# Attention pieces and the projections beside them, issued by a list in the kernel; step projection joined to the values

## The chip, the cores and the metric

The kernel runs on one core of a Trainium2 chip. A core has a matrix engine (TensorE, "PE" in the profile, with its weight loads as "PEld"), VectorE ("DVE"), ScalarE ("ACT"), GpSimd ("POOL") and SyncE ("SP", which here issues nearly all DMAs). Each engine takes its own queue of instructions in the order in which the program was built and stops at an instruction whose semaphores are not there yet. The metric is the device time of one execution in microseconds.

## The reference

One layer of a hybrid diffusion backbone on 512 latent tokens of width 1024, with 256 context tokens. What matters here:

```python
p_lat = h_lat @ w_in                  # columns: z 2048 | xBC 3072 | dt 64 | q 1024 | k 256 | v 256 | gates 2048
p_ctx = h_ctx @ w_in
dt = softplus(dt_raw + dt_bias)       # 2 directions x 32 heads: the "steps" of the state-space scan
q_l, k_l = axial_rope(q), axial_rope(k)
# per block of 128 queries, per KV head (4 query heads each):
logits = concat([q k_win / 8 (+-128 tokens), q k_ctx / 8, sink])
o = softmax(logits) @ [v_win, v_ctx]  # 16 heads of 64, 4 KV heads
out = (sig(g_ssd) * (ssd @ w_o_ssd) + sig(g_att) * (att @ w_o_att)) @ w_out
# then gated residual, ConvFFN, gated residual, final RMSNorm
```

## The kernel before

All large products are made in split precision. A weight piece (128 x 1024, float32, tile `wraw`) is loaded on SP's queue, cast by ACT to `whi` (L149) and its residual made by DVE as `wlo` (L150). `gemm` then issues three matmuls for each of eight slices of the inner dimension: `whi` by the high part, `whi` by the low part, `wlo` by the high part (L192, L193, L195), for 512 latent or 256 context columns. `load` has two buffers each of `whi` and `wlo` and three of `wraw`; `run` goes through a list of steps and loads one piece ahead.

The kernel goes through stages: modulation and norm; keys, queries and values; attention with the z projections beside it; the gates of z, the attention output product (`oa_step`) and the tables of the steps; the state-space scan; the merge; the FFN. The change lies between the values and the attention output product.

Keys and queries. `k_step` and `q_step` make 128 output rows, `rope` rotates them (four quarter copies on ACT, three operations on DVE). `split_k` and `q_split` split the result into high and low halves of a 128-partition tile, by half-tile copies on ACT (L590, L613) and half-tile subtractions on DVE (L591, L614), so that one matmul over 128 partitions multiplies both halves of a query (64 rows high, 64 rows low) by keys doubled on both halves.

Values. `v_step` makes values in token order for six tiles of 128 tokens: 6 tiles x 8 slices x 3 matmuls of 256 columns (L627 to L629), then ACT copies the high part (L634) and DVE makes the residual (L635) in `vst`.

Attention. `block(j, b)` handles KV head j and query block b, 16 in all. For each of four heads: the scores (L669: keys high, keys low, for window and context; into one buffer `score` of two PSUM banks), a masked minimum on DVE (L676, which frees the score buffer), the exponential with its sum on ACT (L680). Then the sums and reciprocals for four heads (L683 to L686), scaling in place on ACT (L689) and DVE (L691). Then for each of 4 or 5 key tiles: four transposes (L698, tile `pt`), high part on ACT (L701), residual on DVE (L702), and two products with the values (L703, L704, tile `po`). At the end ACT copies half of `po` (L706) and DVE adds (L710).

Between blocks stand whole steps: one K step, six Q steps and z steps, given by a table:

```python
    with_ = {(0, 2): [k_step(1)]}
    for j in range(3):
        for b in range(2):
            with_[j, b] = [q_step(2 * j + 2 + b)]
```

A z step (`z_step`) is one product of 512 columns, a tanh on ACT (L520), a multiply on DVE (L522) and a store to DRAM. The framework's scheduler decides how the instructions of neighbouring steps are interleaved on each engine, from its own model of costs, and sets the semaphores.

Steps ("dt"). `dt_tables` first makes its own product with a weight piece of 64 output rows (`gemm(..., m=64)`, 48 matmuls), adds the bias, and computes tables in a long chain of operations on DVE and ACT. It stands behind `att_split` (the split of the attention result into `atth` and `attl`, L837 and L838), three z steps and the first output product; `dt_turn` uses the tables behind the last output product.

Of the kernel before, what the change touches and what calls it, by code (L numbers as in the profile page):

```python
# [44 lines left out]
def tile_hybrid_layer(  # L45
# [14 lines left out]
    wdt: bass.AP,  # L60
# [59 lines left out]
    src["dt", 0] = wdt, 512  # L120
    for i in range(2):
        src["k", i] = wk[i], 1024
        src["v", i] = wv[i], 1024
# [97 lines left out]
    cs_d = dpool.tile([64, L], F32, name="cs_d")  # L221
    tt_d = dpool.tile([64, 4], F32, name="tt_d")
# [351 lines left out]

    def rope(ps, scale):
        sw = tmp("ta")
        for d, s in ((0, 32), (32, 0), (64, 96), (96, 64)):
            S.activation(sw[d : d + 32, :], ps[s : s + 32, :], AF.Copy, scale=scale)
        r = tmp("tb")
        V.scalar_tensor_tensor(r, ps, scale, cosb, ALU.mult, ALU.mult)  # L580
        V.tensor_tensor(sw, sw, sinb, ALU.mult)
        V.tensor_tensor(r, r, sw, ALU.add)
        return r

    def split_k(r, t, lo, hi):
        n = hi - lo
        for u in range(2):
            a, j = 64 * u, 2 * t + u
            for b in (0, 64):
                S.copy(khi[b : b + 64, j, lo:hi], r[a : a + 64, :n])  # L590
                V.tensor_tensor(klo[b : b + 64, j, lo:hi], r[a : a + 64, :n], raw(khi[b : b + 64, j, lo:hi]), ALU.subtract)  # L591

    def k_step(t):
        def fn(w):
            pl, pc = accb(), accb()
            gemm([LAT(pl)], w)
            gemm([CTX(pc)], w)
            split_k(rope(pl, -0.125), t, 0, L)
            rc = tmp("tc")
            S.activation(rc[:, :LC], pc[:, :LC], AF.Copy, scale=-0.125)  # L600
            split_k(rc, t, L, 768)

        return [("k", t)], fn

    Q = {}

    def q_split(ps, t):
        r = rope(ps, 1.0)
        for u in range(2):

            a, b = 64 * u, 64 - 64 * u
            q = a2p.tile([P, L], F32R, tag="q", name="q", bufs=7)
            S.copy(q[a : a + 64, :], r[a : a + 64, :])  # L613
            V.tensor_tensor(q[b : b + 64, :], r[a : a + 64, :], raw(q[a : a + 64, :]), ALU.subtract)  # L614
            Q[2 * t + u] = q

    def v_step(*w):

        pos = [misb() for _ in range(3)]
        for k in range(KT):  # L620
            wh, wl = (z[:, (k % 4) * 256 : (k % 4 + 1) * 256] for z in w[k // 4])
            for p, po in enumerate(pos):
                hh, hl, c0 = (hlh, hll, 2 * p) if p < 2 else (hch, hcl, 0)
                for t in range(2):
                    c = slice((c0 + t) * P, (c0 + t + 1) * P)
                    o = po[:, t * 256 : (t + 1) * 256]
                    T.matmul(o, hh[:, k, c], wh, start=k == 0 and t == 0, stop=False, skip_group_check=True)  # L627
                    T.matmul(o, hh[:, k, c], wl, start=False, stop=False, skip_group_check=True)
                    T.matmul(o, hl[:, k, c], wh, start=False, stop=k == KT - 1, skip_group_check=True)  # L629
        for p, po in enumerate(pos):  # L630
            for t in range(2):
                o = po[:, t * 256 : (t + 1) * 256].rearrange("p (h d) -> p h d", h=4)
                v = vst[:, 2 * p + t, :, :]
                S.copy(v[:, :, 0:64], o)  # L634
                V.tensor_tensor(v[:, :, 64:128], o, raw(v[:, :, 0:64]), ALU.subtract)  # L635
# [11 lines left out]
    run([q_step(1), ([("v", 0), ("v", 1)], v_step)])  # L647
# [3 lines left out]
    def block(j, b, mid=None):  # L651
# [3 lines left out]
        order = con + lat if b == 3 else lat + con  # L655
        n = len(order) * P
        o0 = P if n == 640 else 0
        m = winm[:, 0:512] if b == 3 else winm[:, 896 - n :]
        mneg = a2p.tile([P, 4], F32, tag="mneg", name="mneg", bufs=2)
        den = a2p.tile([P, 4], F32, tag="den", name="den", bufs=2)  # L660
        pts = []
        for i in range(4):
            h = 4 * j + i
            ps = bank("score")
            o = o0
            for z in (con, lat) if b == 3 else (lat, con):
                w = len(z) * P
                for v, k in enumerate((khi, klo)):
                    T.matmul(  # L669
                        ps[:, o : o + w], Q[h][:, b * P : (b + 1) * P], k[:, j, z[0] * P : z[0] * P + w],  # L670
                        start=v == 0 and o % 512 in (0, P), stop=v == 1, skip_group_check=True,
                    )
                o += w
            p = a2p.tile([P, 640], F32, tag="p", name="p", bufs=7)
            mn = mneg[:, i : i + 1]
            V.tensor_tensor_reduce(  # L676
                p[:, :n], ps[:, o0 : o0 + n], m, op0=ALU.add, op1=ALU.min, scale=1.0, scalar=nsink[:, h : h + 1],
                accum_out=mn,
            )
            S.activation(p[:, :n], p[:, :n], AF.Exp, bias=mn, scale=-1.0, accum_out=den[:, i : i + 1])  # L680
            pts.append(p)
        es = a2p.tile([P, 4], F32, tag="es", name="es", bufs=2)
        V.tensor_tensor(es, bcs[:, 32 + 4 * j : 36 + 4 * j], mneg, ALU.add)  # L683
        S.activation(es, es, AF.Exp)
        V.tensor_tensor(es, es, den, ALU.add)
        V.reciprocal(es, es)  # L686
        for i in range(4):
            if i % 2:
                S.activation(pts[i][:, :n], pts[i][:, :n], AF.Copy, scale=es[:, i : i + 1])  # L689
            else:  # L690
                V.tensor_scalar(pts[i][:, :n], pts[i][:, :n], es[:, i : i + 1], None, ALU.mult)  # L691
        if mid:
            mid()
        po = bank("po")
        for c, t in enumerate(order):
            pt = bank("pt")
            for i in range(4):
                T.transpose(pt[:, i * P : (i + 1) * P], pts[i][:, c * P : (c + 1) * P], ident)  # L698
            pth = a2p.tile([P, L], F32R, tag="pth", name="pth", bufs=2)
            ptl = a2p.tile([P, L], F32R, tag="ptl", name="ptl", bufs=2)  # L700
            S.copy(pth, pt)  # L701
            V.tensor_tensor(ptl, pt, raw(pth), ALU.subtract)  # L702
            T.matmul(po, vst[:, t, j, :], pth, start=c == 0, stop=False)  # L703
            T.matmul(po, vst[:, t, j, :], ptl, start=False, stop=c == len(order) - 1)  # L704
        o2 = tmp("tc")
        S.copy(o2[0:64, :], po[64:128, :])  # L706
        po4 = po[0:64, :].rearrange("p (t u q) -> p u t q", t=2, u=2)
        o24 = o2[0:64, :].rearrange("p (t u q) -> p u t q", t=2, u=2)
        for u in range(2):
            V.tensor_tensor(att[64 * u : 64 * u + 64, 2 * j : 2 * j + 2, b * P : (b + 1) * P], po4[:, u], o24[:, u], ALU.add)  # L710
        if b == 3 and j == 0:
            dump("att", att[:, 0, :])

    F = {}
    fill = [z_step(i) for i in range(16)] + [g_step(i) for i in range(NG, 16)]
    n1, n2, n3 = 12, 15, 25

    with_ = {(0, 2): [k_step(1)]}
    for j in range(3):
        for b in range(2):  # L720
            with_[j, b] = [q_step(2 * j + 2 + b)]
# [799 lines left out]
```

## Time and profile before

| | us |
|---|---|
| median of 3 runs | 1292.05 (1290.18 to 1292.60) |
| profiled execution | 1290.21 |
| its span, first to last instruction | 1288.3 |
| PE busy in the span | 1255.9 (97%) |
| DVE busy | 904.5 (70%) |
| ACT busy | 664.7 (52%) |

The profiled execution is the one from which all rows come. Its time is 1.9 us more than its span; the median of the runs is 1.8 us more than its time. In a row of groups, the columns are line, engine, operation, output<-inputs, shape, count, then busy time in us, mean duration in ns, and the idle time of the engine just before, with what ended it. In a timeline row they are start, duration, engine, line, operation, names and count, with the idle time before it in brackets. Ends of matmuls are modelled, and starts are measured: two neighbours' starts tell the pace.

### The profile page before, as it was taken

How to read it: one execution, taken by the hardware profiler on the slowest of the kernel's cores; microseconds unless marked ns; L12 is line 12 of the kernel's file. 1: busy time of each engine (PE TensorE's matmuls, PEld its weight loads, DVE VectorE, ACT ScalarE, POOL GpSimd, SP SyncE). 2: the span in 40 equal slices, each digit the busy share in tenths (PEclk: the TensorE clock that was granted, in tenths of full speed). 3: DMA queues.
4: the chain of work that ended last, by engine and by line, in shares of the span. 5: the costliest groups of instructions: out<-in, count | busy, mean ns of one | idle time of the engine just before them, and what ended most of it. 6: DMA issues, size and time to landing. Idle time of an engine off the chain costs nothing.

```text
span 1288.3 us, 17234 instructions
## 1 busy us (share of the span) xinstructions
PE 1255.9 (97%) x6450; PEld 1022.2 (79%) x6450; DVE 904.5 (70%) x1439; ACT 664.7 (52%) x1230; POOL 132.9 (10%) x113
## 2 busy tenths in 40 slices
PE   7999999999999999999999999999999999999997
PEld 4698777887778878778687787888988888888886
DVE  3867888778495588887887767777677777773323
ACT  3568888767434456375564754223544444442221
POOL 0000000000000033432343430000200000000000
PEclk9999999999999999999999999999999999999999
DMA  8621112121335245444455558777133433333331
GB/s 335 244 92 50 41 58 66 66 74 66 99 127 184 82 107 147 139 119 133 142 131 188 155 168 291 242 244 237 46 113 115 132 114 114 104 109 102 91 102 66
DMA packets 86900, 168.66 MB, mean 131 GB/s; under 512 B 6753, under 2 KB 42081, under 8 KB 86817
## 3 DMA queue, kind: packets, MB, share of 16 engines
q1 hardware_dynamic: 85728, 166.51, 41.2%
q8 instruction: 51, 0.84, 0.3%
q10 hardware_dynamic: 1088, 1.05, 0.2%
q14 instruction: 33, 0.26, 0.1%
HBM read 150.62 MB, written 16.91 MB: 130 GB/s over the span
## 4 chain that ended last, share of the span: by engine, by line
PE 79%; DVE 9%; ACT 5%; DMA 2%; issue 2%; POOL 1%; SPq 0%; DVEq 0%; POOLq 0%; ACTq 0%
PE acc L193 20%; PE acc L192 20%; PE acc L195 20%; PE score L669 2%; PE pt L698 2%; DVE wlo L150 2%; PE mis L1057 2%; PE mis L404 2%; PE po L703 2%; PE mis L1050 1%; PE po L704 1%; ACT whi L149 1%; PE mis L889 1%; PE mis L979 1%; PE acc L1332 1%
## 5 line engine op out<-in xcount | busy, mean ns | idle before, releaser
L150 DVE TENSOR_TENSOR wlo<-wraw,whi 128x1024 fp32r<-128x1024 f32 (+1 forms) x160 | 203.1, 1270 | 132.3 <-ACT whi L149 130.9
L149 ACT CAST whi<-wraw 128x1024 fp32r<-128x1024 f32 (+1 forms) x160 | 165.5, 1036 | 212.7 <-PE acc L193 171.1
L192 PE MATMUL acc<-hlh,whi 128*128 128x512 f32 (+1 forms) x496 | 202.5, 408 | 0.1
L195 PE MATMUL acc<-hlh,wlo 128*128 128x512 f32 (+1 forms) x496 | 195.1, 393 | 0.2 <-DVE wlo L150 0.2
L193 PE MATMUL acc<-hll,whi 128*128 128x512 f32 (+1 forms) x496 | 194.6, 392 | 0.0
L192 PE MATMUL acc<-mh,whi 128*128 128x512 f32 x368 | 143.4, 390 | 0.0
L195 PE MATMUL acc<-mh,wlo 128*128 128x512 f32 x368 | 143.2, 389 | 0.0
L193 PE MATMUL acc<-ml,whi 128*128 128x512 f32 x368 | 143.2, 389 | 0.0
L192 PEld LDWEIGHTS acc<-hlh,whi 128*128 128x128 f32 (+1 forms) x496 | 93.0, 187 | 20.2 <-issue 3.1
L195 PEld LDWEIGHTS acc<-hlh,wlo 128*128 128x128 f32 (+1 forms) x496 | 92.8, 187 | 19.1 <-DVE wlo L150 0.6
L193 PEld LDWEIGHTS acc<-hll,whi 128*128 128x128 f32 (+1 forms) x496 | 93.0, 187 | 18.6 <-issue 2.4
L195 PEld LDWEIGHTS acc<-mh,wlo 128*128 128x128 f32 x368 | 69.1, 188 | 14.5
L192 PEld LDWEIGHTS acc<-mh,whi 128*128 128x128 f32 x368 | 69.1, 188 | 14.2
L193 PEld LDWEIGHTS acc<-ml,whi 128*128 128x128 f32 x368 | 69.1, 188 | 14.2
L963 POOL TENSOR_TENSOR st<-st,eT 128x512 f32<-128x512 f32 x24 | 29.5, 1229 | 424.1 <-ACT st L981 410.6
L245 POOL TENSOR_TENSOR rs<-ms,phalf 128x2 f32<-128x2 f32 (+1 forms) x7 | 6.9, 988 | 544.5 <-DVE ms L244 544.5
L676 DVE CUSTOM_DVE_ANT_0 p<-score,winm,nsink 128x512 f32<-128x512 f32 (+1 forms) x64 | 52.0, 813 | 15.1 <-PE score L669 14.2
L861 ACT ACTIVATE ta<-acc,half 128x512 f32<-128x512 f32 (+1 forms) x66 | 46.5, 704 | 28.3 <-PE acc L195 26.9
L192 PE MATMUL acc<-fh,whi 128*128 128x512 f32 x154 | 60.0, 390 | 0.0
L195 PE MATMUL acc<-fh,wlo 128*128 128x512 f32 x154 | 59.9, 389 | 0.0
L193 PE MATMUL acc<-fl,whi 128*128 128x512 f32 x154 | 59.9, 389 | 0.0
L680 ACT ACTIVATE p<-p,mneg 128x512 f32<-128x512 f32 (+1 forms) x64 | 49.7, 776 | 17.3 <-DVE mneg L676 17.0
(329 smaller groups left out, 2833.0 us busy)
## 6 DMA issues: line engine op xcount, KB each, us to landing
wraw<-wup SPq DMA_DIRECT2D x44, 512.0 KB, 3.5
fb<-cs_d SPq DMA_DIRECT2D x32, 512.0 KB, 6.6
wraw<-wm SPq DMA_DIRECT2D x32, 512.0 KB, 3.7
wraw<-wx SPq DMA_DIRECT2D x24, 512.0 KB, 3.6
wm<-wm SPq DMA_DIRECT2D x16, 512.0 KB, 7.9
wraw<-wz SPq DMA_DIRECT2D x16, 512.0 KB, 3.4
wraw<-wos SPq DMA_DIRECT2D x16, 512.0 KB, 4.5
wraw<-wdn SPq DMA_DIRECT2D x16, 512.0 KB, 3.5
```

Source lines behind the costliest of these rows:

```text
L149: S.copy(hi[:, :n], r[:, :n])
L150: V.tensor_tensor(lo[:, :n], r[:, :n], raw(hi[:, :n]), ALU.subtract)
L192: T.matmul(ps, wh, xh[:, k0 + k, :], start=a, stop=False)
L193: T.matmul(ps, wh, xl[:, k0 + k, :], start=False, stop=False)
L195: T.matmul(ps, wl, xh[:, k0 + k, :], start=False, stop=b)
L404: T.matmul(pg[i], w[a][:, i * P : (i + 1) * P], h[b], start=st and a + b == 0, stop=en and a == 1, skip_group_check=True,)
L669: T.matmul(ps[:, o : o + w], Q[h][:, b * P : (b + 1) * P], k[:, j, z[0] * P : z[0] * P + w], start=v == 0 and o % 512 in (0, P), stop=v == ...
L676: V.tensor_tensor_reduce(p[:, :n], ps[:, o0 : o0 + n], m, op0=ALU.add, op1=ALU.min, scale=1.0, scalar=nsink[:, h : h + 1], accum_out=mn,)
L680: S.activation(p[:, :n], p[:, :n], AF.Exp, bias=mn, scale=-1.0, accum_out=den[:, i : i + 1])
L698: T.transpose(pt[:, i * P : (i + 1) * P], pts[i][:, c * P : (c + 1) * P], ident)
L861: S.activation(o[:, :n], ps[:, :n], AF.Identity, scale=hcol(base_w, stride + i), bias=hcol(base_b, i))
L963: G.tensor_tensor(h8(n), h8(s), bc64(eT[:, z0 : z0 + 8, c]), ALU.mult)
```

## The change

Three things are done.

1. The 64 step columns stand beside the 256 value columns in one weight array. `v_step` now makes 320 columns for each of six token tiles; the step part is copied to a tile, transposed on PE in the attention stage (six transposes), and stored to DRAM. `dt_tables` loads it from there and has no product of its own.
2. Keys and queries are split whole: one copy on ACT and one subtraction on DVE for 128 partitions. DMAs inside SBUF then move the halves to where the scores need them (`k_double`, `q_low`).
3. Attention (16 blocks) and the 19 products beside it (q2 to q7, k1, z0 to z11) are cut into pieces ("atoms"): a score, a minimum, an exponential, a single transpose, a residual, a value product, an eighth of a projection. `plan` sorts the pieces of PE, ACT and DVE into one fixed order, from a table of costs, dependencies and ranks in the kernel. The pieces are issued in that order under a manual schedule, in which the scheduler keeps the order of these pieces on the three engines. Later work that isn't in the list may still be placed between them. Projections have the lowest rank on PE, their weight splits, rotations and gates the highest on ACT and DVE.

The diff, cut to its core:

```diff
     src = {}
-    src["dt", 0] = wdt, 512
+    for i, n in enumerate((3, 3, 2)):
+        src["v", i] = wv[i, :, : n * 320], n * 320
...
+    def k_high(r, t, z):
+        S.copy(khi[:, 2 * t, z], r[:, : z.stop - z.start])
+    def k_low(r, t, z):
+        V.tensor_tensor(klo[:, 2 * t, z], r[:, : z.stop - z.start], raw(khi[:, 2 * t, z]), ALU.subtract)
+    def k_double(t):
+        for k in (khi, klo):
+            for a in (64, 0):
+                nc.sync.dma_start(raw(k[a : a + 64, 2 * t + 1, :]), raw(k[64:128, 2 * t, :]))
+            nc.sync.dma_start(raw(k[64:128, 2 * t, :]), raw(k[0:64, 2 * t, :]))
...
+    def q_high(r, t):
+        q = [a2p.tile([P, L], F32R, tag="q", name="q", bufs=7) for _ in range(2)]
+        S.copy(q[0], r)
+    def q_low(r, t):
+        lo = tmp("tc").bitcast(F32R)
+        V.tensor_tensor(lo, r, raw(q[0]), ALU.subtract)
+        for o, i in ((q[1][64:128, :], q[0][64:128, :]), (q[1][0:64, :], lo[64:128, :]), (q[0][64:128, :], lo[0:64, :])):
+            nc.sync.dma_start(raw(o), raw(i))
...
     def v_step(*w):
-        pos = [misb() for _ in range(3)]
+        pos = [misb() for _ in range(5)] + [accb()]
         for k in range(KT):
+            wh, wl = (z[:, (k % 3) * 320 : (k % 3 + 1) * 320] for z in w[k // 3])
+            for t, po in enumerate(pos):
...
+                T.matmul(o, hh[:, k, c], wh, start=k == 0, stop=False)
+                T.matmul(o, hh[:, k, c], wl, start=False, stop=False)
+                T.matmul(o, hl[:, k, c], wh, start=False, stop=k == KT - 1)
...
+            S.copy(steps[:, t * 64 : (t + 1) * 64], po[:, 256:320])
...
+    def atom(name, engine, cost, needs, rank, emit, whole=True, load=0.11):
+        ATOMS[name] = dict(...)
+    DONE = {"PE": 0.16, "ACT": 0.0, "DVE": 0.0, "DMA": 0.0}
+    NEXT = {"PE": 0.0, "ACT": 0.095, "DVE": 0.083}
+    def plan():
+        todo = {e: sorted((a for a in ATOMS.values() if a["engine"] == e), key=lambda a: a["rank"]) for e in NEXT}
+        free, last, order = {"PE": 0.0, "ACT": 1.6, "DVE": 3.0}, dict.fromkeys(NEXT, (0.0, True)), []
...
+        while any(todo.values()):
+            best = None
+            for e, q in todo.items():
+                one = None
+                for a in q:
+                    r = ready(a)
+                    if r is None:
+                        continue
+                    if one is None or max(r, free[e]) < one[0]:
+                        one = max(r, free[e]), a
+                    if r <= free[e]:
+                        break
+                if one and (best is None or one[0] < best[0]):
+                    best = one
...
+    def block_atoms(n, turned):
...
+            atom("S%d.%d" % (n, i), "PE", 0.83e-3 * w + 0.055, needs, R - 600 + 10 * i, lambda i=i: score(i))
+            atom("r%d.%d" % (n, i), "DVE", 1.09e-3 * w + 0.195, needs, R - 600 + 10 * i, lambda i=i: least(i))
+            atom("e%d.%d" % (n, i), "ACT", 0.83e-3 * w + 0.39, ["r%d.%d" % (n, i)], R - 600 + 10 * i, lambda i=i: exps(i))
...
+                atom("T%s.%d" % (nx, i), "PE", 0.109, needs, R + 100 + 10 * x + i, lambda x=x, i=i: turn(x, i), load=0.055)
+            atom("h" + nx, "ACT", 0.587, needs + (["H" + back] if back else []), R + 100 + 10 * x, lambda x=x: high(x))
+            atom("l" + nx, "DVE", 0.687, ["h" + nx] + (["L" + back] if back else []), R + 100 + 10 * x, lambda x=x: low(x))
+            atom("H" + nx, "PE", 0.227, needs, R + 104 + 10 * x, lambda x=x: values(x, "pth"))
+            atom("L" + nx, "PE", 0.227, needs, R + 105 + 10 * x, lambda x=x: values(x, "ptl"))
+        atom("o%d" % n, "ACT", 0.583, ["L%d.%d" % (n, c - 1)], R + 180, out_low, whole=False)
+        atom("f%d" % n, "DVE", 0.85, ["o%d" % n], R + 180, out_sum, whole=False)
...
+    def product_atoms(g, key, accs):
+        d, R, G_ = {}, 1e6 + 100 * g, "%d" % g
...
+        atom("w" + G_, "ACT", 1.05, was, R - 2e6, high)
+        atom("v" + G_, "DVE", 1.225, ["w" + G_], R - 2e6, low)
...
+            atom("G%s.%d" % (G_, k), "PE", 0.681 if k >= 0 else 0.722, needs, R + k, lambda k=k: piece(k))
...
+        atom("%s%d" % key, "DMA", 6.0, ["z" + G_], R, None)
...
+    BESIDE = [("q", 2), ("q", 3), ("k", 1), ("z", 0), ("z", 1), ("q", 4), ("z", 2), ("z", 3), ("q", 5), ("z", 4)]
+    BESIDE += [("q", 6), ("z", 5), ("z", 6), ("q", 7)] + [("z", i) for i in range(7, 12)]
+    def attention():
...
+        with tc.manual_schedule(engines={mybir.EngineType.PE, mybir.EngineType.Activation, mybir.EngineType.DVE}):
+            for a in plan():
+                a["emit"]()
...
-    def dt_tables(w):
-        pl, pc = accb(), accb()
-        gemm([(pl[:64, :L], hlh, hll), (pc[:64, :LC], hch, hcl)], w, m=64)
+    def dt_tables():
...
+        nc.sync.dma_start(v, dt_d)
+        S.activation(v, v, AF.Identity, bias=dtv[:, 0:1])
...
-    run([([], att_split)] + fill[n1:n2] + oas[:1] + [([("dt", 0)], dt_tables)] + oas[1:] + [([], dt_turn)])
+    run([([], att_split)] + fill[n1:n2] + oas[:1] + [([], dt_tables)] + oas[1:] + [([], dt_turn)])
```

More of the change, by code (lines that the diff above doesn't have):

```diff
@@ L692, in block @@
[L692 to L714, printed above, removed]
+                p[:, :w], d["ps"][i][:, o0 : o0 + w], m, op0=ALU.add, op1=ALU.min, scale=1.0,
@@ new lines, in low, with values, out_low @@
+        def low(x):
+            d["ptl"][x] = a2p.tile([P, L], F32R, tag="ptl", name="ptl", bufs=2)
+            V.tensor_tensor(d["ptl"][x], d["pt"][x], raw(d["pth"][x]), ALU.subtract)
+        def values(x, y):
+            if x == 0 and y == "pth":
+                d["po"] = bank("po")
+            T.matmul(
+                d["po"], vst[:, cols[x], j, :], d[y][x], start=x == 0 and y == "pth", stop=x == c - 1 and y == "ptl"
+            )
+        def out_low():
+            d["o2"] = tmp("tc")
+            S.copy(d["o2"][0:64, :], d["po"][64:128, :])
```

322 lines of the change are left out of this document (233 added, 89 removed).

## The prediction

> **What bounds the kernel now.** I read the page first: busy shares, slices, and the chain that ended last.
>
> ```profile
> span 1288.3 us, 17234 instructions
> ...
> PE 1255.9 (97%) x6450; PEld 1022.2 (79%) x6450; DVE 904.5 (70%) x1439; ACT 664.7 (52%) x1230; POOL 132.9 (10%) x113
> ...
> PE   7999999999999999999999999999999999999997
> ...
> PE 79%; DVE 9%; ACT 5%; DMA 2%; issue 2%; POOL 1%; SPq 0%; DVEq 0%; POOLq 0%; ACTq 0%
> ```
>
> TensorE (PE) carries 79% of the last chain and every slice but the first and last reads 9, so a microsecond counts only if it leaves PE's queue. A busy PE is not a PE at its pace, though: ends are modelled, so short waits hide in "busy". Next come busy times by stretch, cut at the attention stage, the one that the change rewrites.
>
> ```profile
> core 0: us, PE busy (x) PEld busy (x) DVE busy (x) ACT busy (x) POOL busy (x), PEclk, DMA share, GB/s
> 98.20:337.80 239.60, 235.95 (x1242) 189.68 (x1241) 195.08 (x402) 186.00 (x361) 0.00 (x0) 1.00 0.19 62
> ...
> 310.00:324.70 14.70, 12.79 (x67) 9.67 (x66) 10.62 (x22) 10.12 (x21) 0.00 (x0) 1.00 0.11 37
> 324.70:337.80 13.10, 13.10 (x59) 10.88 (x58) 8.73 (x13) 6.64 (x11) 0.00 (x0) 1.00 0.32 99
> ```
>
> The first row runs from the last product of the values to the first attention output product: 239.6 us. To see its waits I need PE's pace, which is the distance from one start to the next. The timeline gives it (start, duration, instruction):
>
> ```profile
> 80.91 0.28 PE L627 MATMUL mis<-whi,hlh 128*128 128x256 f32 x1
> ...
> 98.18 0.40 PE L192 MATMUL acc<-hlh,whi 128*128 128x512 f32 x1
> ...
> 101.61 0.28 PE L669 MATMUL score<-khi,q 128*128 128x256 f32 x1
> ...
> 102.08 0.40 PE L192 MATMUL acc<-hlh,whi 128*128 128x512 f32 x1
> 102.31 0.40 PE L193 MATMUL acc<-hll,whi 128*128 128x512 f32 x1
> ...
> 308.17 1.47 PE L698 MATMUL pt<-ident,p 128*128 128x128 f32 x12
> 309.39 0.36 PE L669 MATMUL score<-khi,q 128*128 128x256 f32 x1
> 309.60 0.50 PE L703 MATMUL po<-pth,vst 128*128 128x512 f32 x1
> ...
> 337.83 0.39 PE L192 MATMUL acc<-atth,whi 128*128 128x512 f32 x1
> ...
> 343.27 0.40 PE L192 MATMUL acc<-hlh,whi 128*64 128x512 f32 x1
> ...
> 351.56 0.40 PE L192 MATMUL acc<-atth,whi 128*128 128x512 f32 x1
> ```
>
> From 337.83 to 343.27 stand 24 matmuls of 512 columns: 0.227 us each. Four of 256 columns fill 101.61 to 102.08: 0.1175 each. Twelve transposes take 1.22 us, and the matmul behind them 0.21 instead of 0.1175: 0.109 per transpose, all told. 384 columns lie midway between 256 and 512: 0.172. The counts of the stretch come from its groups:
>
> ```profile
> L195 PE MATMUL acc<-hlh,wlo 128*128 128x512 f32 x176 | 69.9, 397 | 0.2 <-DVE wlo L150 0.2
> L698 PE MATMUL pt<-ident,p 128*128 128x128 f32 x288 | 43.7, 277 | 1.6 <-ACT p L689 1.2 <-DVE p L691 0.4
> L704 PE MATMUL po<-ptl,vst 128*128 128x512 f32 x72 | 31.4, 436 | 0.3 <-DVE ptl L702 0.3
> L669 PE MATMUL score<-khi,q 128*128 128x256 f32 x96 | 26.5, 290 | 0.3 <-DVE mneg L676 0.3
> L669 PE MATMUL score<-khi,q 128*128 128x384 f32 x32 | 11.8, 368 | 0.2 <-DVE mneg L676 0.2
> L195 PE MATMUL acc<-hch,wlo 128*128 128x256 f32 x8 | 2.3, 292 | 0.0
> ```
>
> Each projection row stands for three (L192, L193, L195), each score row for two (high and low keys), L704 for L703 too. So 3 x 176 + 144 = 672 of 512 columns, 192 + 24 = 216 of 256, 64 of 384, 288 transposes: 152.5 + 25.4 + 11.0 + 31.4 = 220.3 us. The other 19.3 us are waits and stretched starts, though the page calls PE idle for only 3.65. 1.9 of them lie in the end of attention (310 to 324.7: 12.79 busy of 14.70), none behind it (13.10 of 13.10), so 17.4 are spread over the middle. In the built order of instructions (no times in it) PE's first 320 instructions and its last 4,339 are the same in both kernels. Whatever changes lies between 80.91 and 351.56.
>
> **The change part by part.** *Steps beside the values.* The projection of the steps, 48 matmuls from 343.27 to 351.56, goes: -8.3 us. The 144 matmuls of the values (80.91 to 98.18, 0.120 each) grow from 256 to 320 columns. No row shows 320; between 0.120 and 0.172 (384) the midpoint is 0.146, so +3.8, with ends at 0 (0.120) and +7.5 (0.172). Six transposes are new: +0.65. Net -3.9, between -7.7 and -0.2. The way of the steps through DRAM I cost at nothing. The load is issued by SP behind the last value product, and the table work can start behind the attention split, some 10 us earlier against its users than before, under eight output products of 5.44 us. Without that cover the store and load stand on the path.
>
> *Keys and queries split whole, halves moved by DMA.* This frees DVE and ACT, none of it on PE. The transfers of the queries queue on SP between weight loads and gate stores. The first needed late are those of q5, and products in between hide 2 to 3 us each:
>
> ```profile
> cs_d<-du SPq DMA_DIRECT2D x1, 128.0 KB, 2.3
> ```
>
> No transfer inside SBUF is in the trace; this store of the same size is nearest. I take zero; if each of the six came 2 us late, +12, which I leave to the upper end.
>
> *The fixed order.* The chains of ACT and DVE are the same work, at these prices:
>
> ```profile
> L702 DVE TENSOR_TENSOR ptl<-pt,pth 128x512 fp32r<-128x512 f32 x72 | 47.4, 687 | 13.5 <-ACT pth L701 12.5 <-PE pt L698 0.3 <-PE po L704 0.3
> L150 DVE TENSOR_TENSOR wlo<-wraw,whi 128x1024 fp32r<-128x1024 f32 x27 | 33.0, 1222 | 9.0 <-ACT whi L149 8.6 <-issue 0.2
> L676 DVE CUSTOM_DVE_ANT_0 p<-score,winm,nsink 128x512 f32<-128x512 f32 x32 | 23.8, 745 | 7.6 <-PE score L669 7.0 <-PE pt L698 0.3
> L149 ACT CAST whi<-wraw 128x1024 fp32r<-128x1024 f32 x27 | 28.3, 1049 | 11.3 <-PE acc L193 9.2 <-issue 1.1 <-ACT p L680 0.8
> L837 ACT CAST atth<-att 128x512 fp32r<-128x512 f32 x8 | 4.3, 619 | 0.0
> L838 DVE TENSOR_TENSOR attl<-att,atth 128x512 fp32r<-128x512 f32 x8 | 4.9, 685 | 0.0
> ```
>
> The list's constants are these rows (three matmuls 0.681, weight split 1.225, residual 0.687), so its order should come near what the engines do: a score, turn or value product where its operand is due, eighths of a projection in between. Place by place:
>
> Start. In the built order, the second weight split stands on DVE ahead of the first masked minimum, and the second score waits for that minimum. After the last value product: about 1.0 to the last copy, 1.05 cast, 1.22 residual, 0.75 + 0.1 minimum: 4.1 us. PE has one score (0.47) and three eighths (2.04) beside it: +1.6 that was not there (0 to 4).
>
> Middle. Stretched starts stay: 102.08 to 102.31 is 0.231, not 0.227, over some 670 matmuls 2.6 us. No slack is left between a minimum and the score behind it, so I allow 0.06 for each of 64: 3.8. Together 6.4 where 17.4 were. Bounds: 2.6 and 17.4.
>
> End. The projections in the list run out before the last two blocks. The next z product, not in the list, is dealt by the scheduler into that end: 21 of its matmuls, 4.8 us, stand ahead of the last value product. They cover unevenly: 2.5 us of waits against 1.9 (0 to 6.7, if they covered nothing).
>
> Handover. Behind the last value product ACT has a copy (0.6), the eight casts (4.3), a tanh (0.6) and the next weight cast (1.05), then DVE that weight's residual (1.22): 6.6 and about 8.4 us. PE has 27 matmuls (6.1) and four more (0.9) to cover it: +2.0 (0 to 3), where before there were none, since the z product then began earlier. Here the casts are on the path.
>
> Waits: 1.6 + 6.4 + 2.5 + 2.0 = 12.5 against 19.3, so -6.8. With the work, -10.7. The profiled execution took 1290.21 us (span 1288.3 and 1.9 around it), so 1279.5. The median of the runs shown, 1292.05, lies 1.8 higher: 1281.4.
>
> **The rivals.** *The waits only move.* The middle keeps its 17.4 us, because no product is ever as fine as the gap that it should fill. For it: before, a scheduler also dealt products into the gaps. Against it: whole columns of transposes then stood together, where the list places single ones. Waits 23.5, work -3.9: +0.3, 1292.4, no difference.
>
> *Splits hold the minimum (slower).* The list ranks weight splits above everything, and DVE cannot pass one. Before, at the same place (timeline, ACT and DVE):
>
> ```profile
> 99.86 0.39 ACT L634 CAST vst<-mis 128x256 fp32r<-128x256 f32 x1
> 100.01 1.22 DVE L150 TENSOR_TENSOR wlo<-wraw,whi 128x1024 fp32r<-128x1024 f32 x1 [0.47 <-ACT whi L149]
> 101.15 0.42 DVE L635 TENSOR_TENSOR vst<-mis,vst 128x256 fp32r<-128x256 f32 x1
> ```
>
> The last value tile was copied at 100.25, its residual waited 0.9 us behind the split, and the first score began at 101.61, just after it. In the built order nine of the 19 splits stand directly ahead of a minimum and most others ahead of a residual. Each can hold PE, which goes on in a fixed order, by up to 1.22 us. One is in my sum. If 13 of the other 18 do, +15.9: 1297.3; from nine on (10.7 / 1.22) there is no gain. [...] Against the rival: DVE is busy for 195 of 239.6 us, and eighths of a product can stand where the list knows a split to be.
>
> *All of it comes.* The middle falls to 2.6 and the end is covered: waits 6.2, work -3.9, 1275.0.
>
> **How the numbers follow.** The forecast gets 0.68, unchanged waits 0.12, holding splits 0.12, all of it 0.08. The range leaves out the holding splits and a part of each of the other two rivals (0.05 and 0.02), and takes in the ends of the value columns and of the handover: 1274.5 to 1292.5. About 0.2% (2.6 us) is what a measurement can tell from no change, so faster means under 1289.5. To faster go the forecast, all of it, and 0.02 of the unchanged waits: 0.78. The same keeps 0.10, slower 0.12.
>
> **What would show it.** Right: no matmul with 64 output rows behind attention; 144 value matmuls at 0.143 to 0.149; a stop of 1 to 2 us between the first two scores; the stretch from the last value product to the first attention output product near 233 us and the output products from there on without the 8.3 us. Wrong: stops of about 1.2 us at scores ended by a masked minimum whose DVE predecessor is a weight split; scores ended by a query transfer; a granted clock under 1.00; a handover over 3 us.

## The result and the profile after

The changed kernel took 1277.72 us (median of 4 runs, 1276.86 to 1278.44), the kernel before 1291.38 beside it: a ratio of 0.989, 95% interval 0.988 to 0.991, or 13.7 us less. The forecast was 1281.4. In a second measurement the ratio was 0.988 (0.986 to 0.990). The profiled execution took 1278.44.

The page of the changed kernel: span, busy time by engine, and the shares of the chain that ended last.

```profile
span 1276.6 us, 17208 instructions
...
PE 1244.3 (97%) x6408; PEld 1022.4 (80%) x6408; DVE 890.0 (70%) x1419; ACT 655.3 (51%) x1217; POOL 132.8 (10%) x113
...
PE 67%; issue 13%; DVE 9%; DMA 5%; ACT 3%; POOL 1%; SPq 0%; DVEq 0%; POOLq 0%; ACTq 0%
```

TensorE (PE) is still busy for 97% of a shorter span, and has 42 matmuls fewer. Where the time went is told by the same starts as in the prediction (timeline: start, duration, instruction):

```profile
81.42 0.30 PE L654 MATMUL mis<-whi,hlh 128*128 128x320 f32 x1
...
102.53 0.28 PE L759 MATMUL score<-khi,q 128*128 128x256 f32 x1
...
319.87 0.40 PE L808 MATMUL po<-ptl,vst 128*128 128x512 f32 x1
...
327.61 0.50 PE L191 MATMUL acc<-atth,whi 128*128 128x512 f32 x1 [0.21 <-ACT whi L148]
...
338.60 0.39 PE L191 MATMUL acc<-atth,whi 128*128 128x512 f32 x1
```

From the first value matmul to the first matmul of the second attention output product it was 80.91 to 351.56, 270.65 us; now it is 81.42 to 338.60, 257.18. So 13.5 us leave this stretch (called the stage below). What lies ahead is 0.5 us longer and what lies behind 1.3 us longer (936.8 to 938.1): the span is 11.7 us shorter.

The 144 value matmuls take 21.11 us, 0.1466 each. The groups of the stage keep the counts of the kernel before (one row of them):

```profile
L191 PE MATMUL acc<-hlh,whi 128*128 128x512 f32 x176 | 71.4, 406 | 0.3 <-ACT whi L148 0.3
```

With the same work, what is left are waits and stretched starts. I add up, over neighbouring PE starts from the first score to the end of the stage, the distance less the pace of the earlier instruction (0.227, 0.172, 0.1175 and 0.109 us, as in the prediction): 19.3 us before, 9.6 after. The sum by place: 1.1 in the first 3.5 us, 4.3 up to 302 us, 2.8 to the last value product, 1.5 behind it. Busy times by stretch (middle, end, handover) say the same:

```profile
core 0: us, PE busy (x) PEld busy (x) DVE busy (x) ACT busy (x) POOL busy (x), PEclk, DMA share, GB/s
106.15:302.00 195.85, 195.58 (x1091) 167.59 (x1092) 160.14 (x337) 157.08 (x307) 0.00 (x0) 1.00 0.27 86
302.00:320.10 18.10, 17.31 (x93) 13.23 (x92) 14.30 (x32) 13.42 (x27) 0.00 (x0) 1.00 0.14 45
320.10:342.00 21.90, 21.29 (x92) 16.66 (x90) 20.77 (x24) 13.32 (x20) 0.00 (x0) 1.00 0.38 130
```

In the middle PE is idle for 0.27 of 195.85 us; the other 4 us of the sum are starts a little late behind a PE that counts as busy. All that PE visibly waits for between 102 and 342 us stands in four lines (waits: total, times, longest):

```profile
PE score L759 <- DVE mneg L768: 1.3, 3, 0.9
PE acc L191 <- ACT whi L148: 0.5, 2, 0.3
PE po L808 <- ACT pth L799: 0.2, 1, 0.2
PE pt L795 <- ACT p L788: 0.2, 1, 0.2
```

No line names a transfer of queries or keys.

The same sum, sorted by the matmul that starts late, tells where the 9.7 us were gained. At value products it falls from 6.0 us to nothing (-0.2), at transposes from 6.5 to 3.3; at projections it is 4.1 and 3.9, at scores 2.8 and 2.6. So nearly all of the gain lies at transposes and value products, and none at the scores behind a minimum. What these matmuls waited for shows best at their weight loads (PEld), whose stops aren't hidden in a modelled end; a load starts ahead of its matmul, by a median of 0.18 us before and 0.22 after, so the totals are larger than PE's own: 8.0 us against 0.7 for `pth` before (all from 102 to 342 us; waits before, then after):

```profile
PEld po L703 <- ACT pth L701: 8.0, 27, 0.7
PEld pt L698 <- DVE p L691: 3.4, 11, 0.6
PEld pt L698 <- ACT p L689: 2.9, 8, 1.4
PEld score L669 <- DVE mneg L676: 2.4, 10, 0.3
PEld po L704 <- DVE ptl L702: 2.4, 9, 0.6
```

```profile
PEld score L759 <- DVE mneg L768: 2.2, 3, 1.3
PEld po L808 <- ACT pth L799: 1.4, 3, 0.7
...
PEld pt L795 <- ACT p L788: 1.2, 4, 0.4
...
PEld pt L795 <- DVE p L790: 0.5, 1, 0.5
```

Waits for the high part of the transposes (`pth`), for their residual (`ptl`) and for the scaled exponentials (`p`) were 16.7 us at the loads and are 3.1; those for a minimum stay.

### The profile page after: what moved, and what is told of

Its sections match the earlier page's. It is cut to its first block, busy times and chain, and to the rows that moved or that the text cites. A ratio compares the mean times of both kernels' runs of the same rounds, so it can differ in the third digit from the quotient of the medians.

```text
span 1276.6 us, 17208 instructions
## 1 busy us (share of the span) xinstructions
PE 1244.3 (97%) x6408; PEld 1022.4 (80%) x6408; DVE 890.0 (70%) x1419; ACT 655.3 (51%) x1217; POOL 132.8 (10%) x113
## 4 chain that ended last, share of the span: by engine, by line
PE 67%; issue 13%; DVE 9%; DMA 5%; ACT 3%; POOL 1%; SPq 0%; DVEq 0%; POOLq 0%; ACTq 0%
PE acc L194 16%; PE acc L192 16%; PE acc L191 16%; PE score L759 2%; PE po L808 2%; PE pt L795 2%; DVE wlo L149 2%; PE mis L404 2%; PE mis L1312 2%; PE mis L1305 1%; DMA ld<-ao_d 1%; DMA ld<-yz_d 1%; DMA wraw<-wm 1%; DMA zs<-zs_d 1%; PE acc L1587 1%
## 5 line engine op out<-in xcount | busy, mean ns | idle before, releaser
L149 DVE TENSOR_TENSOR wlo<-wraw,whi 128x1024 fp32r<-128x1024 f32 (+1 forms) x141 | 179.9, 1276 | 128.7 <-ACT whi L148 122.1
L148 ACT CAST whi<-wraw 128x1024 fp32r<-128x1024 f32 (+1 forms) x141 | 145.5, 1034 | 202.9 <-PE acc L192 149.6
L191 PE MATMUL acc<-hlh,whi 128*128 128x512 f32 x488 | 201.2, 412 | 0.3 <-ACT whi L148 0.3
L192 PE MATMUL acc<-hll,whi 128*128 128x512 f32 x488 | 191.3, 392 | 0.0
L194 PE MATMUL acc<-hlh,wlo 128*128 128x512 f32 x488 | 191.1, 392 | 0.1
L194 PEld LDWEIGHTS acc<-hlh,wlo 128*128 128x128 f32 x488 | 91.7, 188 | 20.8 <-DVE wlo L149 0.6
L191 PEld LDWEIGHTS acc<-hlh,whi 128*128 128x128 f32 x488 | 91.9, 188 | 18.5 <-issue 3.1
L192 PEld LDWEIGHTS acc<-hll,whi 128*128 128x128 f32 x488 | 92.0, 189 | 18.1 <-issue 2.4
L775 ACT ACTIVATE p<-p,mneg 128x512 f32<-128x512 f32 (+1 forms) x64 | 49.6, 776 | 19.1 <-DVE mneg L768 18.8
```

The lines of the kernel that those rows point to most:

```text
L148: S.copy(hi[:, :n], r[:, :n])
L149: V.tensor_tensor(lo[:, :n], r[:, :n], raw(hi[:, :n]), ALU.subtract)
L191: T.matmul(ps, wh, xh[:, k0 + k, :], start=a, stop=False)
L192: T.matmul(ps, wh, xl[:, k0 + k, :], start=False, stop=False)
L194: T.matmul(ps, wl, xh[:, k0 + k, :], start=False, stop=b)
L775: S.activation(p, p, AF.Exp, bias=d["mneg"][:, i : i + 1], scale=-1.0, accum_out=d["den"][:, i : i + 1])
```

## The experiments

The change has three parts: the joined steps, the whole splits and the fixed order. All runs in one table; "stage" and "waits" are taken as above from each kernel's own profiled execution. Differences of the stage are sharper than those of the medians, which carry 0.1 to 0.3% of uncertainty each: the changed kernel, profiled twice, has 257.2 and 257.3. Where the scheduler deals an order (before, e1, e4 and e5, and for some engines e6 and e6b), a row shows the one order that it dealt, and its waits say nothing sure of another.

| kernel | median, us | ratio to before (95%) | stage, us | waits, us |
|---|---|---|---|---|
| before | 1291.38 | 1 | 270.7 | 19.3 |
| changed | 1277.72 | 0.989 (0.988 to 0.991) | 257.2 | 9.6 |
| e1 joined steps alone | 1292.44 | 1.000 (0.999 to 1.001) | 273.3 | 25.8 |
| e2 changed, steps not joined | 1284.63 | 0.993 (0.991 to 0.995) | 261.5 | 9.5 |
| e3 changed, half-tile splits | 1283.66 | 0.993 (0.992 to 0.995) | 264.3 | 16.7 |
| e4 changed, no fixed order | 1285.27 | 0.994 (0.992 to 0.995) | 264.9 | 15.5 |
| e5 whole splits alone | 1295.53 | 1.002 (1.001 to 1.004) | 273.9 | 22.5 |
| e6 order on PE alone | 1286.35 | 0.995 (0.994 to 0.997) | 266.3 | 18.8 |
| e6b order on ACT and DVE alone | 1277.84 | 0.989 (0.986 to 0.993) | 258.0 | 8.7 |
| e7 whole products as pieces | 1325.42 | 1.025 (1.022 to 1.028) | 303.1 | 55.6 |
| f0 changed again | 1277.34 | 0.988 (0.986 to 0.990) | 257.3 | 9.8 |
| f1 start | 1277.42 | 0.989 (0.987 to 0.990) | 257.1 | 9.5 |
| f2 start, handover | 1279.65 | 0.990 (0.988 to 0.992) | 255.5 | 7.9 |
| f3 start, handover, end | 1279.20 | 0.990 (0.988 to 0.992) | 255.2 | 7.6 |

### One part alone, and one part taken back

**e1, joined steps alone.** The steps of 320 columns go into the kernel before; their six transposes stand where the product of the steps stood.

```diff
-        gemm([(pl[:64, :L], hlh, hll), (pc[:64, :LC], hch, hcl)], w, m=64)
+        st = ep.tile([P, 768], F32, tag="d6", name="dst")
+        nc.sync.dma_start(st[:, :384], st_d)
+        for t in range(6):
+            o = pl[:64, t * P : (t + 1) * P] if t < 4 else pc[:64, (t - 4) * P : (t - 3) * P]
+            T.transpose(o, st[:, t * 64 : (t + 1) * 64], ident)
```

> The kernel before with the joined steps alone: 320 columns for the values, the steps kept, six transposes in place of the product of the steps, no list and no whole splits. First theory (the change's 13.7 us are 3.9 us of work from the joined steps and 9.7 us of waits that the fixed order of pieces takes out): 3.9 us less than the kernel before, 1287.5, with 144 value matmuls at 0.147 us each. Rival (the product of the steps stood where the engine would have waited anyway, so that joining frees nothing and the wider values are pure cost): 1291 to 1295. Rival (the joining starts the tables earlier and is worth most of the change): below 1283.

Measured 1292.4: no gain. The 3.8 us of work are gone, but the waits grew by 6.4. The attention code is that of the kernel before; the scheduler only dealt it anew. Its largest stop (timeline, left out lines lie between):

```profile
150.04 2.84 DVE L591 TENSOR_TENSOR klo<-tb,khi 64x512 fp32r<-64x512 f32 x4
...
153.16 1.77 DVE L591 TENSOR_TENSOR klo<-tc,khi 64x256 fp32r<-64x256 f32 x4 [0.28 <-ACT khi L590]
...
154.96 0.75 DVE L675 CUSTOM_DVE_ANT_0 p<-score,winm,nsink 128x512 f32<-128x512 f32 x1
...
155.78 0.39 PE L668 MATMUL score<-khi,q 128*128 128x256 f32 x1 [2.67 <-DVE mneg L675]
```

The key's eight subtractions were dealt ahead of a masked minimum whose scores stood ready, and the next score waited 2.67 us. The first rival gave the right figure, for a wrong reason: no wait had stood where the steps' product stood.

**e2, the changed kernel without the joined steps.** `v_step`, `dt_tables` and the weights are those of the kernel before; `turn_atoms` is left out.

> The changed kernel without the joined steps: 256 columns of values in two weight pieces, the steps' own product of 64 rows behind the first attention output product, no transposes of the steps; list and whole splits stay. First theory: 3.9 us more than the changed kernel, 1281.6. Rival (product of the steps covered by a wait of the handover): 1274 to 1278. Rival (joining is worth most of the change): above 1286.

Measured 1284.6, by ratios 4.4 to 5.8 us more than the changed kernel's two measurements, each with some 3 us of uncertainty. The stage settles it: 4.3 us longer, of which 3.8 are work and 0.7 a pause between the last value matmul and the first score that the changed kernel doesn't have; the waits from there on are 9.5 against 9.6. The rest of the difference lies outside the stage. So the joined steps pay what the rows say as long as the order around them is fixed.

**e3, the changed kernel with half-tile splits**, with their costs in the list:

```diff
+            subs = [(lambda f, u=u: f(d["rp"], t, u), 0.617, 0.685) for u in range(2)]
...
+            subs = [(lambda f, u=u: f(d["rp"], t, KL, u), 1.24, 1.37) for u in range(2)]
+            subs += [(lambda f, u=u: f(d["rc"], t, KC, u), 0.81, 0.836) for u in range(2)]
```

> The changed kernel with keys and queries split in half tiles by ScalarE and VectorE as before, no transfers inside SBUF; the list knows the longer costs (a query 1.23 us on ScalarE and 1.37 on VectorE in place of 0.62 and 0.69, the key 4.1 and 4.4 in place of 0.95 and 1.05). First theory (the order takes out the waits, the splits are beside PE): within 1.5 us of the changed kernel, 1277 to 1279.2, waits of the middle 4 to 6 us. Rival (relief of the two engines takes out the waits): most of the 9.7 us back, 1283 to 1287.

Measured 1283.7, which is the rival's figure. But over the first 150 us from the first score on the waits are 4.6 us against 3.6: relief of the engines is worth 1 us there. Most of the rest lies in one place near the end (timeline):

```profile
303.14 1.23 DVE L149 TENSOR_TENSOR wlo<-wraw,whi 128x1024 fp32r<-128x1024 f32 x1 [0.79 <-ACT whi L148]
...
304.29 0.68 DVE L901 SCALAR_TENSOR_TENSOR te<-tb,acc 128x512 f32<-128x512 f32 x1
...
304.88 0.84 DVE L813 TENSOR_TENSOR att<-po,tc 64x256 f32<-64x256 f32 x2
...
305.76 0.88 DVE L761 CUSTOM_DVE_ANT_0 p<-score,winm,nsink 128x640 f32<-128x640 f32 x1
...
306.70 0.58 PE L752 MATMUL score<-khi,q 128*128 128x256 f32 x1 [3.44 <-DVE mneg L761]
```

The scheduler put the weight residual of a product that isn't in the list (L149 is the residual that `load` makes) on DVE; the list's own gate and addition follow, and only then the minimum, whose scores had started by 302.98. PE stood for 3.44 us, and its granted clock was 0.50 for 6.8 us from 305.76 on (last section). This is the second rival of the prediction at work, at a place where the list doesn't rule. Whether every order of half-tile splits would meet it was not tried.

**e4, the changed kernel without the manual schedule**; the pieces are emitted in the same sequence.

```diff
-        with tc.manual_schedule(engines={mybir.EngineType.PE, mybir.EngineType.Activation, mybir.EngineType.DVE}):
-            for a in plan():
-                a["emit"]()
+        for a in plan():
+            a["emit"]()
```

> The changed kernel with the same pieces emitted in the same sequence, but without the manual schedule: the framework's scheduler may place them as it does in the kernel before. First theory (the fixed order, not the pieces, takes out the waits): waits near the old 19 us, 1285 to 1289. Rival (pieces, joined steps and whole splits suffice, the scheduler finds as good an order from them): 1276 to 1280.

Measured 1285.3, at the lower edge of the theory: the stage is 7.7 us longer. Its waits from the first score on are 5.9 us more than with the order, some of it at half clock (3.41 us long, last section); 1.8 more lie ahead of the first score, where the scheduler put the transposes of the steps first, and they wait for a copy on ACT. But 15.5 is 3.8 less than before: a part of the gain came in this deal without the order, so the theory has the larger part right and not all of it.

**e5, whole splits alone** in the kernel before.

> The kernel before with the whole splits alone (one copy and one subtraction for 128 partitions, transfers inside SBUF); steps, table of steps and scheduler as before. Theory after the first four runs (the scheduler's order is a draw: waits of the stage were 19.3, 25.8 and 15.5 us in three kernels whose PE work differs by 3.9 us at most): 1287 to 1299 with waits of 15 to 26 us, and no relation to the relieved engines. Rival (whole splits take out the stops behind the key's eight subtractions, and that is where the waits were): 1282 to 1286.

Measured 1295.5, 0.24% slower than before (0.06 to 0.41): the rival falls. The waits of 22.5 us hold one stop of 4.06 us at the last block's transposes. In the order that was dealt here, whole splits bring nothing by themselves.

### Which engine's order it is

**e6 and e6b** keep the order on some engines only:

```diff
-        with tc.manual_schedule(engines={mybir.EngineType.PE, mybir.EngineType.Activation, mybir.EngineType.DVE}):
+        with tc.manual_schedule(engines={mybir.EngineType.PE}):                                       # e6
+        with tc.manual_schedule(engines={mybir.EngineType.Activation, mybir.EngineType.DVE}):         # e6b
```

> The changed kernel with the manual schedule on TensorE alone; ScalarE's and VectorE's pieces are dealt by the scheduler. Theory (all three orders have to fit, since a score waits for a minimum that stands in VectorE's order): waits between the 9.6 us of the changed kernel and the 15.5 without an order, 1280 to 1284. Rival (PE's order alone counts, the other two have slack): 1277 to 1279.

> The changed kernel with the manual schedule on ScalarE and VectorE, and TensorE's pieces dealt by the scheduler. Theory (all three have to fit): 1280 to 1285. Rival (the order of the two small engines is what counts): 1277 to 1279.

I had both wrong. The order on PE alone gives 1286.4, no better than no order at all; the order on ACT and DVE alone gives 1277.8, the changed kernel's time, though the scheduler deals PE's pieces. Its stage is 0.8 us longer, all of it at the start.

That doesn't show that PE's order is of no account, for the scheduler dealt PE almost the list's own. Of PE's 1195 matmuls behind the last value matmul up to the last value product, taken in order of start by line, names and shape, 1175 stand in the changed kernel's sequence in e6b, 1036 of them in one unbroken run; in e4 it is 1091. In e6 1190 do, but on DVE only 332 of 373 and on ACT 298 of 339 (372 and 338 in e6b). So PE's order alone isn't enough; with the order of ACT and DVE PE's came out by itself, the pieces being emitted in the list's sequence. Whether a quite different order on PE would do as well was not tried. The waits of PE (e6 first, its two largest lines, then e6b):

```profile
PE score L759 <- DVE mneg L768: 4.2, 9, 0.9
PE po L808 <- ACT pth L799: 1.4, 5, 0.5
```

```profile
PE pt L960 <- ACT te L662: 1.6, 1, 1.6
PE pt L795 <- ACT p L788: 0.9, 2, 0.7
PE acc L191 <- ACT whi L148: 0.7, 1, 0.7
PE po L808 <- ACT pth L799: 0.2, 1, 0.2
```

With the order on ACT and DVE no score's wait for a minimum is listed any more. In e6 nine are, and two of the longest look alike (timeline of e6):

```profile
201.73 1.22 DVE L886 TENSOR_TENSOR wlo<-wraw,whi 128x1024 fp32r<-128x1024 f32 x1
...
202.87 0.74 DVE L768 CUSTOM_DVE_ANT_0 p<-score,winm,nsink 128x512 f32<-128x512 f32 x1
...
203.68 0.38 PE L759 MATMUL score<-khi,q 128*128 128x256 f32 x1 [0.50 <-DVE mneg L768]
...
231.80 1.22 DVE L886 TENSOR_TENSOR wlo<-wraw,whi 128x1024 fp32r<-128x1024 f32 x1 [0.73 <-ACT whi L883]
...
234.48 0.45 PE L759 MATMUL score<-khi,q 128*128 128x384 f32 x1 [0.65 <-DVE mneg L768]
```

Both times a weight residual stands on DVE ahead of the minimum (the second time with a z step's multiply in between): the second rival's mechanism once more. The changed kernel does the same, and PE doesn't wait (timeline of the changed kernel):

```profile
255.54 0.28 PE L759 MATMUL score<-klo,q 128*128 128x256 f32 x1
...
257.63 1.22 DVE L886 TENSOR_TENSOR wlo<-wraw,whi 128x1024 fp32r<-128x1024 f32 x1
...
258.76 0.74 DVE L768 CUSTOM_DVE_ANT_0 p<-score,winm,nsink 128x512 f32<-128x512 f32 x1
...
260.45 0.39 PE L808 MATMUL po<-pth,vst 128*128 128x512 f32 x1
...
260.69 0.28 PE L759 MATMUL score<-khi,q 128*128 128x256 f32 x1
```

The minimum starts 3.2 us after its scores, behind a residual, and PE goes on without a gap: until 260.45 it has eighths of a product and transposes, and the next score comes 1.2 us after the minimum's end. Over the stage, a residual of a weight stands directly ahead of 8 of the 64 minima in the changed kernel and of 5 before. Minima don't start sooner after their scores: 1.24 us on average behind the start of the last of a head's four score matmuls, against 1.14 (1.68 against 1.70 behind the first). What differs is the distance from a minimum's end to the next score: under 0.2 us in 4 of 63 cases, against 13 before, 12 in e4, 11 in e6, 18 in e1 and 3 in e6b. A score that stands right behind the minimum is a score that has waited or nearly so. The order of the two small engines doesn't make the minimum prompt; it sees to it that it is seldom later than PE can spare. That tells e6 and e1 from the changed kernel; against the kernel before, as shown above, the gain is at the transposes and value products, which the same two engines feed.

**e7, whole projections as pieces**: one piece of 24 matmuls in place of eight.

```diff
-            atom("G%s.%d" % (G_, k), "PE", 0.681 if k >= 0 else 0.722, needs, R + k, lambda k=k: piece(k))
+            cost = 0.681 * 8 if lo_ >= 0 else 0.722 * 4
+            atom("G%s.%d" % (G_, hi_), "PE", cost, needs, R + lo_, lambda a=lo_, b=hi_: [piece(k) for k in range(a, b + 1)])
```

> The changed kernel, but each projection is one piece of 24 matmuls (5.45 us) in the list in place of eight pieces of 0.68 us; rules, costs and ranks stay. Theory (the fine pieces are what fills the gaps of about 1 us between a score and the next): a block's four scores and minima need about 5.7 us in a chain, one product covers at most one minimum, and the 4 us of transposes and values cover the rest in part: 1 to 2 us of new waits in each of 16 blocks, 1293 to 1310. Rival (an order that knows the costs does as well with whole products): 1277 to 1281.

Measured 1325.4, worse than the theory's upper end. PE's longest waits are for minima (up to 345 us):

```profile
PE score L759 <- DVE mneg L768: 17.1, 22, 2.0
PE po L808 <- ACT pth L799: 5.1, 11, 1.1
```

34 of 63 scores stand within 0.2 us of their minimum. The waits are 46 us more where the theory had 16 to 32. It left out that half clock followed some of the waits, see below: in the five stretches of 50 us from 100 us on the granted clock was 0.97, 1.00, 0.90, 0.93 and 0.97, by my estimate from these up to 12 us of the 46.

### What is left

**f1, f2, f3** take on the three waits that the profile after shows, one more each time: the second weight residual behind the first minimum; the last two z products ahead of the attention split; a thirteenth z product in the list.

```diff
-        atom("v" + G_, "DVE", 1.225, ["w" + G_], R - 2e6, low)
+        atom("v" + G_, "DVE", 1.225, ["w" + G_] + (["r0.0"] if g == 1 else []), R - 2e6, low)
...
-    run([([], att_split)] + fill[n1:n2] + oas[:1] + [([], dt_tables)] + oas[1:] + [([], dt_turn)])
+    run(fill[n1:n1 + 2] + [([], att_split)] + fill[n1 + 2 : n2] + oas[:1] + [([], dt_tables)] + oas[1:] + [([], dt_turn)])
...
-    BESIDE += [("q", 6), ("z", 5), ("z", 6), ("q", 7)] + [("z", i) for i in range(7, 12)]
+    BESIDE += [("q", 6), ("z", 5), ("z", 6), ("q", 7)] + [("z", i) for i in range(7, 13)]
```

> The changed kernel with one edge more in the list: the second weight residual on VectorE stands behind the first masked minimum. Theory (the stop of 1.07 us between the first two scores comes from that residual alone): stop under 0.1, 1.0 us less than the changed kernel, nothing else moves. Rival (the residual then holds the second minimum, and the stop moves to the third score): within 0.3 us of it.

The stop at the second score falls from 1.07 to 0.58, other waits up to 152 us grow by 1.4, those behind 252 us fall by 0.7: nothing in all (1277.4). The rival had the outcome, if not the place.

> As the run before, and the last two z products in front of the attention split in the list of steps, so that their weight casts stand in ScalarE's queue ahead of the eight casts of the split. Theory (the 1.5 us of waits in the handover come from casts queued behind the split): 0.7 to 1.4 us less again, 2 us less than the changed kernel in all. Rival (the split itself then comes late and the first output product waits for it): 0 to 2 us more.

The handover's 1.5 us go to 0, as the theory said. But the kernel isn't faster (1279.7). The waits of PE up to 400 us tell a part of the reason:

```profile
PE acc L194 <- DVE wlo L149: 2.1, 2, 1.9
```

The second output product begins 2.2 us earlier (336.40), the tables of the steps on DVE don't to the same degree, and a weight residual of the output products stands behind them: that wait was 0.94 us in the changed kernel and is 1.93 now. A longer wait took back a part of it, 25 us later (in the kernel before it was 0.95, so it isn't new). In the profile of f2 the granted clock is 0.99 between 600 and 900 us, far behind the stage, where that of the changed kernel has 1.00; no run shows that the edit is its cause.

> As the run before, and the thirteenth z product in the list. Theory (2.6 us of waits between 293 and 310 us come from the list running out of products): 1 to 2.5 us less again. Rival (the product that then no longer stands free is missed at the end, the waits move behind the last score): within 0.5 us.

The end (252 us to the last value product) keeps 3.5 of 4.6 us of waits, but the wait behind the tables grows to 2.3 us, and 3.41 us at half clock follow (363.33 to 366.74, granted clock 0.50). No gain (1279.2). No version that I ran is faster than the changed kernel by more than the uncertainty.

## Why the prediction was right, point by point

- *Work, -3.9.* Right: 0.1466 per value matmul against 0.146, no product of the steps behind attention, e2. That the way through DRAM costs nothing was right too: the first wait behind the tables is 0.94 us, and 0.95 before. But the sum took it as certain in any order, and e1 shows that the same edit without the fixed order returned all of it in new waits.
- *Start, +1.6.* Measured 1.1, with the cause that was named: the residual at 104.20, the minimum at 105.34, the second score at 106.15 after a wait of 0.91.
- *Middle, 6.4.* Measured 4.3. This is the term that was mis-sized, and both of its parts are wrong. The allowance of 0.06 us for each of 64 scores (3.8) came to nothing: at the 59 scores behind a minimum in the middle the sum is -0.9 us, since the next score nearly always stands well behind the minimum. All other starts hold 5.2 where 2.6 were forecast; projection matmuls behind one another alone hold 3.7 (367 starts, 0.010 each and not 0.004). That the middle comes near is in part luck. Where its waits stood before, the sum didn't ask: at the scores behind a minimum they were 0.6 of 16.2 us. The remark against the first rival, that whole columns of transposes stood together, came closer than the sum.
- *End, 2.5; handover, 2.0.* Measured 2.8 and 1.5. The prediction took the end before from idle time (1.9), but all else from starts; by starts the end before held 3.2. In the handover the listed times up to the residual add up to 7.8 us, not to "about 8.4"; against PE's 7.0 us of cover they give 0.8 and not 2.0, so that this term comes near is in part luck. f2 shows that the casts of the split were the handover's cause.
- *The sum.* Waits 9.6 for 12.5, work as forecast: -13.5 in the stage for -10.7. Against that, 0.5 us ahead of it and 1.3 behind it were not in the sum. The profiled execution is 1278.44 for 1279.5; the median lies 0.7 under it, where I had put it 1.8 above. So 3.7 us of error: 2.9 in waits, 2.6 in that offset, less 1.8.
- *The argument for the fixed order* was half right. I had laid the gain to PE's order ("a score, turn or value product where its operand is due"). e6 shows that PE's order alone doesn't bring it, e6b that the order of ACT and DVE does, with PE's following almost of itself. The eighths that I named as cover are needed (e7), but once ACT and DVE are fixed the scheduler places them on PE nearly as the list does.
- *The rivals.* That waits only move: no, they halved; but f2 and e1 show the effect within one experiment each. *Splits hold the minimum*: the mechanism is there, 8 times in the changed kernel, and costs PE 0.5 to 3.4 us at a place in e6 and e3; it didn't decide, because in the changed kernel PE had other pieces each time but at the start. A hold of up to 1.22 us at each of many splits, as the prediction counted it for this rival, did not come: one of the 8 is a stop, of 0.91 us. DVE itself kept the order there: the residual of 104.20 takes 1.23 us, and the minimum behind it, whose four scores had started by 102.89, starts at 105.34.
- *Query transfers at zero.* Right: no PE wait is ended by one.

## What to carry to other kernels

When one engine is the bound and two others feed it, first fix the order on the feeders; here the bound engine, cut into pieces of well under a microsecond and emitted in a good sequence, could then be left to the scheduler, while its order alone was worth nothing (e6). Don't ask whether a long operation stands ahead of a needed one, ask how much other work the bound engine still has at that moment: the distance from the feeder's end to the next use shows it. And a saving in work that was measured inside a fixed order may vanish under a scheduler that deals anew: compare stage by stage before calling an edit useless.

## What the runs showed of the hardware

After some waits of PE its clock was at half as well, so that they cost twice. In e1 the granted clock falls to half for 3.41 us after the stop of 2.67 us, in f3 after one of 2.3, but in f2 not after one of 1.93; in e7 it is 0.50 from 146.84 to 150.25, behind 3.41 us in which PE was busy for 1.34. Busy times by stretch for e1, e4 and f2 (e1 and e4 cut where the clock changes, f2 at the end of its stop):

```profile
153.27:156.68 3.41, 0.73 (x4) 0.53 (x4) 3.29 (x7) 3.31 (x7) 0.00 (x0) 1.00 0.00 0
156.68:160.09 3.41, 3.18 (x10) 2.70 (x11) 2.79 (x6) 0.95 (x4) 0.00 (x0) 0.50 0.50 184
```

```profile
308.81:312.22 3.41, 1.77 (x10) 1.07 (x8) 3.24 (x9) 3.39 (x8) 0.00 (x0) 1.00 0.21 79
312.22:315.63 3.41, 2.89 (x14) 2.89 (x15) 2.43 (x7) 1.55 (x3) 0.00 (x0) 0.50 0.51 154
```

```profile
357.79:361.20 3.41, 1.48 (x8) 0.91 (x6) 3.27 (x8) 1.38 (x2) 0.00 (x0) 1.00 0.36 108
361.20:364.61 3.41, 3.41 (x15) 2.84 (x16) 3.30 (x5) 1.32 (x2) 0.00 (x0) 1.00 0.68 133
```

Where a stretch of half clock was measured whole, it lasted 3.41 us (e1, e4, f3) or twice that: 6.83 in e3 and, by the mean clock of its stretches, about 6.9 in e5, from within stops of 3.44 and 4.06. How long PE was busy in the 3.41 us ahead doesn't settle whether it comes: 0.73 and 1.77 us were followed by half clock (e1, e4), 1.48 was not (f2), so its condition stays open here. In e3 starts of 256 columns stand 0.21 us apart at half clock (307.09, 307.30 and 307.51) for 0.1175; my estimate from this is that a half-clock stretch full of matmuls loses some 1.5 of its 3.41 us. In the stage of the changed kernel and of the kernel before it never came (granted clock 1.00 in both).
